# Attention loop of an mLSTM block: loads of the next head ordered behind all splits, output end behind the next weighing

## The chip, the core and the metric

The kernel runs on one core of a Trainium2 chip as one launch. Its time is device time in microseconds (us), as the median of several runs; the profile is one further execution under the hardware profiler. The engines are named as in the profile: PE (matrix multiplications; its weight loads are PEld), DVE (VectorE), ACT (ScalarE), POOL (GpSimd) and SP (SyncE, which here only starts DMAs).

## What is computed

One layer of a diffusion backbone on 512 latent tokens of width 1024 with 256 context tokens. Its parts are an adaLN-modulated RMSNorm, two token mixers on the normalised input (a bidirectional mLSTM with 4 heads of 256 and a Hyena long convolution), a gated merge, an output projection and a SwiGLU. The change lies in the mLSTM. For one head and one direction it is, chunk by chunk:

```python
b = cumsum(log_f)
logD = where(tril, b[t] - b[s] + log_i[s], NEG)
m_t = max(b + m, max(logD))
s = einsum("td,sd->ts", q, k) * exp(logD - m_t)
num = einsum("ts,sd->td", s, v) + a * einsum("vk,tk->tv", C, q)
den = sum(s) + a * einsum("k,tk->t", n, q)
h = num / max(abs(den), exp(-m_t))
```

The kernel does it without chunks: for a head, six blocks of 128 keys (four latent, two of the context), all at once, with a decay weight for each block, query and direction. Then each head is normalised over its 256 channels, multiplied by an output gate, and goes to the next projection.

## The kernel before, in words

All matrix products are made of fp32 values split into a high and a low half. `split` (L214) lets ACT copy the high half (L215) and DVE subtract it to get the low half (L216); `mm3` (L233) then makes a product of three matmuls: high by high (L234), high by low (L235), low by high (L236). Raw tiles come by SP's DMAs into a buffer "wr", of which there are four (L182); a load of the next raw tile can start when the split of the tile four before it is done.

The loop over the heads (from L1373) runs, for head h (0 to 3; the third head is h = 2), in this order:

- `load_head(h + 1)` (L912) starts the loads of Q (one tile) and K (two halves) of the next head and splits them into uh, ul and K. They are traced inside `issued_behind(weighed)`, which orders their instructions, on each engine, behind the last multiply of the weighing of head h; it adds no wait.
- `values(h, 0)` (L970) multiplies the weighted scores of the forward direction by V (vh, vl): four output tiles, each followed by the small division steps (ACT L981 and L985, DVE L982, L983).
- `decay(h + 1, 1)` (L874) fills four banks by matmuls (L882, L884), and ACT makes exponentials of them into the tiles dx and dy (L888); `decay(h + 1, 0)` was traced before it.
- `beside` (L1361) adds an independent piece: a tile of the Hyena projection wph (`ph_tiles`, L1318; a load into "wr", its split into wh and wl, 24 matmuls, a DVE step L1326, a store), and steps over the modulation weights wada (L373, on DVE, from the same four buffers).
- `late` (L1367) is the output end of head h - 1 (`head_out`, L1006): eight transposes on PE into two banks (L1011), an ACT copy of each bank (L1014), a DVE step with the gate (L1015), a split (ACT L220, DVE L221) and stores.
- `weigh(h + 1)` (L949): six products of six matmuls of K and Q; after each, two DVE multiplies (L961) put the scores into the exponentials (tiles dx and dy) and free the bank. Products, decay and output end share one set of four banks; `values` and the wph tile have four others.
- `values(h, 1)` for the backward direction, then `load_values(h + 1)` (L926, V of the next head), `halves` (L964, the splits of dx and dy), another `beside`, and `head_norm` (L989, with a power on POOL, L997).

The order on each engine is what the scheduler makes of this code: it goes by the order written, the priorities and the `issued_behind` and `behind` marks. Each engine runs its own list in order, so an instruction that waits holds up all that stand behind it on that engine.

Of the kernel before, what the change touches and what calls it, by code (L numbers as in the profile page):

```python
# [160 lines left out]
def build(nc, tc, I, out, dbg=None):  # L161
# [24 lines left out]
    def T(p, shape, dt=F32, tag=None, bufs=None):  # L186
        uid[0] += 1
        p = HOME.get(tag, p)
        bufs = BUFS.get(tag, bufs)
        kw = {} if bufs is None else {"bufs": bufs}  # L190
        nm = f"{tag or 't'}_{uid[0]}"
        return p.tile(list(shape), dt, tag=tag or nm, name=nm, **kw)
# [9 lines left out]
    def bank(p=None):  # L202
        return T(p or psH, [128, 512], F32, "bank")
# [10 lines left out]
    def split(hi, lo, x):  # L214
        act.activation(hi, x, AF.Copy)  # L215
        dve.tensor_sub(lo, x, hi.bitcast(F32))  # L216
# [16 lines left out]
    def mm3(o, wh, wl, xh, xl, first, last):  # L233
        pe.matmul(o, wh, xh, start=first, stop=False)  # L234
        pe.matmul(o, wh, xl, start=False, stop=False)  # L235
        return pe.matmul(o, wl, xh, start=False, stop=last)  # L236
# [342 lines left out]
    def behind(lag=0):  # L579

        return tc.issue_after(tails[-1 - lag])
# [285 lines left out]
    def parts(dt=F32):  # L867
        return T(PM_, [128, 10, 128], dt, "dy"), T(PM_, [128, 8, 128], dt, "dx")

    def piece(w, d, s):  # L870
        t0, n, i, off = PIECE[d][s]
        return w[i][:, off : off + n]
# [32 lines left out]
    def staged(src, n, hi, lo, a=None):  # L905
        t = T(PW, [128, WMAX], F32, "wr")[:, :n]
        if a:
            t = t.rearrange("p (a b) -> p a b", a=a)
        dma(t, src)
        split(hi, lo, t)  # L910

    def load_head(h):  # L912

        kh, kl = (T(PT, [128, 2048], F32R, "K")[:, :1536].rearrange("p (a b) -> p a b", a=2) for _ in range(2))
        qh, ql = T(PT, [128, 2, SEQ], F32R, "uh"), T(PT, [128, 2, SEQ], F32R, "ul")

        staged(qd[:, 2 * h : 2 * h + 2], 2 * SEQ, qh[:], ql[:], 2)
        if h == 0:
            fill(next(cf))
        for i in range(2):  # L920
            staged(kd[:, 2 * h + i], SEQ + CTX, kh[:, i], kl[:, i])
        return (qh, ql), (kh, kl)

    weighed, valued = [], []

    def load_values(h):  # L926
        Vh, Vl = T(PM_, [128, 6, NV], F32R, "vh"), T(PM_, [128, 6, NV], F32R, "vl")
        gp.memset(Vh[:, :, 256:257].bitcast(F32), 1.0)
        gp.memset(Vh[:, :, 257:258].bitcast(F32), 0.0)
        gp.memset(Vl[:, :, 256:258].bitcast(F32), 0.0)  # L930
        n0 = len(nc.cur_bb.bb.instructions)
        for b, n in ((0, 4), (4, 2)):
            staged(vd[:, h, b : b + n], 256 * n, Vh[:, b : b + n, :256], Vl[:, b : b + n, :256], n)
        valued[:] = last_of(nc.cur_bb.bb.instructions[n0:])
        return Vh, Vl

    def last_of(traced):

        ends = {i.engine: i for i in traced if i.engine in (nc.vector.engine, nc.scalar.engine)}
        return list(ends.values())  # L940

    @contextmanager
    def issued_behind(ends):
        with ExitStack() as stack:
            for i in ends:
                stack.enter_context(tc.issue_after(i))
            yield

    def weigh(h, qq, kk, Dm):  # L949

        (qh, ql), (kh, kl) = qq, kk
        for s in (4, 5, 0, 1, 2, 3):
            ps = bank()
            tk = slice(128 * s, 128 * s + 128)
            for i in range(2):
                mm3(ps[:], kh[:, i, tk], kl[:, i, tk], qh[:, i], ql[:, i], i == 0, i == 1)
            for d in range(2):
                t0, n = PIECE[d][s][:2]
                dst = piece(Dm[d], d, s)
                sv = ps[:, 128 * t0 : 128 * (t0 + n)].rearrange("p (a b) -> p a b", a=n)  # L960
                m = dve.scalar_tensor_tensor(dst, sv, 1.0 / 64, dst, op0=ALU.mult, op1=ALU.mult)  # L961
        weighed[:] = [m.ins]

    def halves(Dm):  # L964
        wh, wl = parts(F32R), parts(F32R)
        for i in (1, 0):
            split(wh[i][:], wl[i][:], Dm[i][:])
        return wh, wl

    def values(h, d, W, V, den, hs):  # L970
        (wh, wl), (Vh, Vl) = W, V
        for t in range(4):
            ps = bank(psG)
            src = [4, 5] + [s for s in range(4) if (s <= t if d == 0 else s >= t)]
            for j, s in enumerate(src):
                b = t - PIECE[d][s][0]
                m = mm3(ps[:, :NV], piece(wh, d, s)[:, b], piece(wl, d, s)[:, b], Vh[:, s], Vl[:, s], j == 0, j == len(src) - 1)
            tails.append(m.ins)
            dn = den[:, d, t : t + 1]
            with tc.high_priority(PR[0]):  # L980
                act.activation(dn, ps[:, 256:257], AF.Abs)  # L981
                dve.tensor_tensor(dn, dn, G["em"][:, d, t, h : h + 1], op=ALU.max)  # L982
                dve.reciprocal(dn, dn)  # L983
                if d == 0:
                    act.activation(hs[:, t], ps[:, :256], AF.Copy, scale=dn)  # L985
                else:
                    dve.scalar_tensor_tensor(hs[:, t], ps[:, :256], dn, hs[:, t], op0=ALU.mult, op1=ALU.add)
# [12 lines left out]
    def head_gate(h):  # L1000
        o = [T(PM_, [128, SEQ], F32, "s2") for _ in range(2)]
        for i in range(2):
            dma(o[i][:], od[:, 2 * h + i])
        return o
# [223 lines left out]
    def fill(n):  # L1228
        for _ in range(n):
            if fills:  # L1230
                fills.pop(0)()
# [72 lines left out]
    def reload(src, hi, lo, ks=range(KT)):  # L1304
        xs = ([], [])
        for k in ks:
            xs[0].append(hi())
            xs[1].append(lo())
            load_halves(xs[0][-1][:], xs[1][-1][:], both(src, k))
        return xs  # L1310
# [20 lines left out]
    L = load_head(0)  # L1331
    fill(next(cf))
    V = load_values(0)
    sel = T(PM_, [128, 32], F32R, "sel")
# [9 lines left out]
    def steps(n):  # L1344
        for _ in range(n):
            background()

    Dm = [decay(0, d) for d in range(2)]
    fill(next(cf))
    weigh(0, L[0], L[1], Dm)  # L1350
    fill(next(cf))
    W = [halves(Dm[d]) for d in range(2)]
    fill(next(cf))
# [7 lines left out]
    def beside(h, i):  # L1361
        for _ in range(PHN[h][i]):
            with issued_behind(valued if i == 0 else ()):
                next(ph)
        steps(ST[h])

    def late(keep=False):  # L1367
        if done:
            with behind():
                ends.extend(head_out(*done.pop(), keep))  # L1370

    ends = []
    for h in range(NH):  # L1373
        last = h == NH - 1
        den = T(PM_, [128, 2, 4], F32, "den", 2)
        hs = T(PM_, [128, 4, 256], F32, "hs", 2)
        if last:
            sp_ = [T(PT, [128, 2048], F32R, "K") for _ in range(2)]
            parts_ = [[v[:, 512 * j : 512 * j + 512] for j in range(4)] for v in sp_]
            for i, tag in enumerate(("uh", "ul")):  # L1380
                v = T(PT, [128, 2, SEQ], F32R, tag)
                parts_[i] += [v[:, 0], v[:, 1]]
            its = [iter(v) for v in parts_]
            hm = reload(hmd, lambda: next(its[0]), lambda: next(its[1]), range(4))
        else:
            with issued_behind(weighed):
                L = load_head(h + 1)
            with behind():
                D0 = decay(h + 1, 0)
        values(h, 0, W[0], V, den, hs)  # L1390
        if not last:
            with behind():
                Dm = D0, decay(h + 1, 1)
            if h == 0:
                fill(len(fills))
            beside(h, 0)
            late()
            weigh(h + 1, L[0], L[1], Dm)
        values(h, 1, W[1], V, den, hs)
        if last:  # L1400
            late(True)
        else:
            V = load_values(h + 1)
            W = [halves(Dm[d]) for d in range(2)]
            beside(h, 1)
        with tc.high_priority(PR[0] if last else 0):
            head_norm(hs)
        done.append((h, hs, head_gate(h)))
# [8 lines left out]
    with behind():  # L1417
        ends = head_out(*done.pop(), True)
# [369 lines left out]
```

## Time and profile before

| | |
|---|---|
| runs, median of 3 | 1206.57 us (1204.78 to 1208.85) |
| the profiled execution's own time | 1202.72 us |
| its span | 1201.0 us |
| PE busy | 1167.7 us, 97% |
| DVE busy | 933.1 us, 78% |
| ACT busy | 561.8 us, 47% |
| POOL busy | 92.3 us, 8% |

PE is busy in almost every slice of the span, so the profile is read from what PE waits for. The granted clock has a mean of 0.995 of full speed (2.4 GHz). Busy times of the other engines are averages over stages: in the attention loop DVE is nearly full.

### The profile page before, as it was taken

To read this page: it belongs to the slowest core of one execution; us is meant where nothing else is said; L and a number is where in the kernel's file an instruction comes from. 1 tells how busy PE (TensorE), PEld (TensorE's weight loads), DVE (VectorE), ACT (ScalarE), POOL (GpSimd) and SP (SyncE) were. 2 spreads that over 40 slices of the span, in tenths; PEclk is the share of its full clock that TensorE was granted. 3 is DMA by queue.
4 is the path that set the end of the run, shared out by engine and by line. 5 is a ranking of instruction groups with operands and counts; after the bars stand their busy time and mean duration, and the time that the engine had idled before them with its cause. 6 is when DMAs were issued, how large, how long until landed. Compare 5 with 4: busy or idle time off the path is not lost.

```text
span 1201.0 us, 18193 instructions
## 1 busy us (share of the span) xinstructions
PE 1167.7 (97%) x6992; PEld 1028.5 (86%) x6992; DVE 933.1 (78%) x1503; ACT 561.8 (47%) x875; POOL 92.3 (8%) x175
## 2 busy tenths in 40 slices
PE   4999999999999999999999999999999999999997
PEld 2799988988888888888788988879999999998886
DVE  6967798987989999899648887685878987897332
ACT  3763465754554455444756643233433443362221
POOL 0011110110000010101132131000000000000000
PEclk9899999999999999999999999999999999999998
DMA  9745343454245342434685587793323323357312
GB/s 344 258 141 178 142 163 117 143 207 155 86 140 184 115 153 93 175 110 136 215 257 180 175 252 239 261 328 134 121 71 105 106 83 111 106 185 248 98 49 70
DMA packets 64135, 193.31 MB, mean 161 GB/s; under 512 B 8872, under 2 KB 12720, under 8 KB 61488
## 3 DMA queue, kind: packets, MB, share of 16 engines
q1 hardware_dynamic: 51536, 150.20, 37.5%
q0 software_dynamic: 12512, 41.95, 9.8%
q8 instruction: 55, 0.90, 0.3%
q14 instruction: 32, 0.26, 0.1%
HBM read 156.47 MB, written 35.65 MB: 160 GB/s over the span
## 4 chain that ended last, share of the span: by engine, by line
PE 86%; DMA 5%; DVE 5%; issue 1%; ACT 1%; POOL 1%; SPq 0%; DVEq 0%; POOLq 0%; ACTq 0%
PE bank L234 25%; PE bank L235 25%; PE bank L236 24%; DMA wr<-in_wada 2%; PE bank L1558 2%; PE bank L661 2%; PE bank L662 2%; PE bank L663 2%; DVE wl L216 1%; DVE wr L373 1%; DMA mats<-in_mats 1%; PE bank L617 1%; PE bank L464 1%; PE bank L465 1%; DMA hb<-in_dftf 1%
## 5 line engine op out<-in xcount | busy, mean ns | idle before, releaser
L215 ACT ACTIVATE wh<-wr 128x1024 fp32r<-128x1024 f32 (+3 forms) x195 | 195.1, 1005 | 340.8 <-PE bank L235 224.1
L234 PE MATMUL bank<-hTh,wh 128*128 128x512 f32 (+1 forms) x912 | 338.2, 372 | 2.0 <-ACT hTh L1113 2.0
L235 PE MATMUL bank<-hTl,wh 128*128 128x512 f32 (+1 forms) x912 | 337.8, 370 | 2.2 <-DVE hTl L1119 2.2
L236 PE MATMUL bank<-hTh,wl 128*128 128x512 f32 (+1 forms) x912 | 337.1, 370 | 0.0
L216 DVE TENSOR_TENSOR wl<-wr,wh 128x1024 fp32r<-128x1024 f32 (+3 forms) x195 | 223.1, 1153 | 98.6 <-ACT wh L215 96.9
L234 PEld LDWEIGHTS bank<-hTh,wh 128*128 128x128 f32 x912 | 172.9, 190 | 29.6 <-ACT hTh L1113 2.2
L235 PEld LDWEIGHTS bank<-hTl,wh 128*128 128x128 f32 x912 | 172.8, 189 | 29.1 <-DVE hTl L1119 2.5
L236 PEld LDWEIGHTS bank<-hTh,wl 128*128 128x128 f32 x912 | 172.7, 189 | 28.2
L235 PE MATMUL bank<-big,wh 128*128 128x256 f32 (+1 forms) x314 | 101.6, 324 | 1.2 <-DVE big L216 1.2
L234 PE MATMUL bank<-big,wh 128*128 128x256 f32 (+1 forms) x314 | 101.9, 324 | 0.2 <-ACT big L215 0.2
L236 PE MATMUL bank<-big,wl 128*128 128x256 f32 (+1 forms) x314 | 101.4, 323 | 0.0
L235 PEld LDWEIGHTS bank<-big,wh 128*128 128x128 f32 x314 | 59.8, 190 | 6.4 <-DVE big L216 1.8
L234 PEld LDWEIGHTS bank<-big,wh 128*128 128x128 f32 x314 | 59.7, 190 | 5.4 <-ACT big L215 0.8
L236 PEld LDWEIGHTS bank<-big,wl 128*128 128x128 f32 x314 | 59.7, 190 | 4.5
L373 DVE SCALAR_TENSOR_TENSOR wr<-wr,crow 128x1024 f32<-128x1024 f32 x32 | 38.7, 1221 | 23.4 <-DMA wr<-in_wada 23.3
L215 ACT ACTIVATE hb<-hb 128x512 fp32r<-128x512 f32 (+1 forms) x49 | 36.5, 767 | 32.9 <-DVE hb L469 18.1
L234 PE MATMUL bank<-uh,wh 128*128 128x256 f32 (+1 forms) x164 | 51.1, 311 | 0.0
L235 PE MATMUL bank<-ul,wh 128*128 128x256 f32 (+1 forms) x164 | 51.1, 311 | 0.0
L236 PE MATMUL bank<-uh,wl 128*128 128x256 f32 (+1 forms) x164 | 51.1, 311 | 0.0
L216 DVE TENSOR_TENSOR hb<-hb,hb 128x512 fp32r<-128x512 f32 (+1 forms) x49 | 40.5, 860 | 2.0 <-ACT hb L215 1.8
L663 PE MATMUL bank<-wh,hTl 128*128 128x256 f32 (+1 forms) x128 | 36.4, 284 | 0.0
L661 PE MATMUL bank<-wh,hTh 128*128 128x256 f32 (+1 forms) x128 | 36.4, 284 | 0.0
(407 smaller groups left out, 2418.0 us busy)
## 6 DMA issues: line engine op xcount, KB each, us to landing
wr<-in_win SPq DMA_DIRECT2D x64, 512.0 KB, 3.6
wr<-in_w SPq DMA_DIRECT2D x60, 512.0 KB, 3.5
wr<-in_wada SPq DMA_DIRECT2D x32, 512.0 KB, 4.7
Kd<-K POOLq DMA_DIRECT2D x8, 1024.0 KB, 4.7
K<-Kd SPq DMA_DIRECT2D x8, 1024.0 KB, 6.3
wr<-in_wv SPq DMA_DIRECT2D x8, 512.0 KB
gmd<-s POOLq DMA_DIRECT2D x16, 256.0 KB, 2.5
wr<-in_wph SPq DMA_DIRECT2D x8, 512.0 KB, 3.8
```

The source lines that it names most:

```text
L215: act.activation(hi, x, AF.Copy)
L216: dve.tensor_sub(lo, x, hi.bitcast(F32))
L234: pe.matmul(o, wh, xh, start=first, stop=False)
L235: pe.matmul(o, wh, xl, start=False, stop=False)
L236: return pe.matmul(o, wl, xh, start=False, stop=last)
L373: dve.scalar_tensor_tensor(w, w, 1.0, crow[:], op0=ALU.mult, op1=ALU.mult, accum_out=s)
L464: pe.matmul(ps[:], lhs, w4h, start=True, stop=False)
L465: pe.matmul(ps[:], lhs, w4l, start=False, stop=True)
L661: pe.matmul(o, xh, wh, start=bool(k == 0), stop=False)
L662: pe.matmul(o, xh, wl, start=False, stop=False)
L663: m = pe.matmul(o, xl, wh, start=False, stop=bool(k == KT - 1))
L1558: m = pe.matmul(ps, w[:, k], half(h2[x][k], hf), start=n == 1, stop=n == 3 * KT)
```

## The change

`halved` holds the last ACT and the last DVE instruction of the V load and of `halves` of a head. The next iteration orders its Q and K loads' instructions behind these too; for h = 0 it is empty, so the loads of head 1 keep their place and those of heads 2 and 3 move. And `late()` is called after `weigh(h + 1)`; that moves something for h = 1 and h = 2.

```diff
--- before.py
+++ after.py
@@ -1369,7 +1369,7 @@
             with behind():
                 ends.extend(head_out(*done.pop(), keep))
 
-    ends = []
+    ends, halved = [], []
     for h in range(NH):
         last = h == NH - 1
         den = T(PM_, [128, 2, 4], F32, "den", 2)
@@ -1383,7 +1383,7 @@
             its = [iter(v) for v in parts_]
             hm = reload(hmd, lambda: next(its[0]), lambda: next(its[1]), range(4))
         else:
-            with issued_behind(weighed):
+            with issued_behind(weighed + halved):
                 L = load_head(h + 1)
             with behind():
                 D0 = decay(h + 1, 0)
@@ -1394,14 +1394,16 @@
             if h == 0:
                 fill(len(fills))
             beside(h, 0)
+            weigh(h + 1, L[0], L[1], Dm)
             late()
-            weigh(h + 1, L[0], L[1], Dm)
         values(h, 1, W[1], V, den, hs)
         if last:
             late(True)
         else:
+            n0 = len(nc.cur_bb.bb.instructions)
             V = load_values(h + 1)
             W = [halves(Dm[d]) for d in range(2)]
+            halved = last_of(nc.cur_bb.bb.instructions[n0:])
             beside(h, 1)
         with tc.high_priority(PR[0] if last else 0):
             head_norm(hs)
```

No instruction is added or removed. DVE at the second head (h = 1), in the order before. vl is the V of that head, wl the tile of wph, K the second half of K of the third head:

```order
L216 TENSOR_TENSOR vl_6180<-wr_6188,vh_6179 128x2x256
L216 TENSOR_TENSOR wl_6445<-wr_6443,wh_6444 128x1024
L1326 SCALAR_TENSOR_TENSOR s_1074_6246<-s_1074_6246,bank_6248 128x512
L996 TENSOR_SCALAR rs_6277<-mv_6276 128x1
L994 BN_STATS bst_6283<-hs_5886 128x6
L216 TENSOR_TENSOR K_6314<-wr_6325,K_6313 128x768
```

The wph tile is split right behind V, K follows. The same place in the changed kernel:

```order
L216 TENSOR_TENSOR K_6314<-wr_6325,K_6313 128x768
L982 TENSOR_TENSOR den_6311<-den_6311,em_1972 128x1
L995 BN_AGGR mv_6292<-bst_6291 128x2
L994 BN_STATS bst_6299<-hs_5886 128x6
L983 RECIPROCAL den_6311<-den_6311 128x1
L996 TENSOR_SCALAR rs_6293<-mv_6292 128x1
L995 BN_AGGR mv_6300<-bst_6299 128x2
L373 SCALAR_TENSOR_TENSOR wr_6478,modT_78<-wr_6478,crow_5518 128x1024
L216 TENSOR_TENSOR wl_6445<-wr_6443,wh_6444 128x1024
```

wl has moved behind the second half of K, small division and norm steps and a wada step (L373).

ACT at the same place, before; dy and dx are the exponentials of the third head:

```order
L215 ACTIVATE vh_6179<-wr_6188 128x2x256
L215 ACTIVATE wh_6444<-wr_6443 128x1024
L888 ACTIVATE dy_6329<-bank_6331,ad_1908 128x128 x4
L888 ACTIVATE dx_6330<-bank_6338,ax_1910 128x512 x2
L981 ACTIVATE den_6311<-bank_6349 128x1
```

The exponentials follow one another. In the changed kernel:

```order
L215 ACTIVATE vh_6179<-wr_6188 128x2x256
L888 ACTIVATE dy_6329<-bank_6331,ad_1908 128x128 x3
L215 ACTIVATE K_6313<-wr_6325 128x768
L888 ACTIVATE dy_6329<-bank_6331,ad_1908 128x128
L981 ACTIVATE den_6311<-bank_6349 128x1
L888 ACTIVATE dx_6330<-bank_6338,ax_1910 128x512 x2
L985 ACTIVATE hs_6312<-bank_6349,den_6311 128x256
L981 ACTIVATE den_6311<-bank_6363 128x1
L215 ACTIVATE wh_6444<-wr_6443 128x1024
```

The second half of K is split between them, and wh has moved behind a part of the exponentials.

DVE at the third head (h = 2), before; s are tiles of the output end, dx the exponentials of the fourth head, wl tiles of wph:

```order
L1326 SCALAR_TENSOR_TENSOR s_1195_6874<-s_1195_6874,bank_6876 128x512
L216 TENSOR_TENSOR wl_7381<-wr_7379,wh_7380 128x1024
L1015 SCALAR_TENSOR_TENSOR s_1200_6916<-s_1165_6732,s_1200_6916 128x512
L1015 SCALAR_TENSOR_TENSOR s_1201_6923<-s_1166_6733,s_1201_6923 128x512
L961 SCALAR_TENSOR_TENSOR dx_6755<-bank_6930,dx_6755 128x512
L221 TENSOR_TENSOR s_1200_6916<-s_1200_6916,s_1165_6732 128x512
L221 TENSOR_TENSOR s_1201_6923<-s_1201_6923,s_1166_6733 128x512
L961 SCALAR_TENSOR_TENSOR dx_6849<-bank_6930,dx_6849 128x512
L961 SCALAR_TENSOR_TENSOR dx_6755<-bank_6939,dx_6755 128x512
L961 SCALAR_TENSOR_TENSOR dx_6849<-bank_6939,dx_6849 128x512
L216 TENSOR_TENSOR wl_7419<-wr_7417,wh_7418 128x1024
```

The output end stands in front of the multiplies. In the changed kernel:

```order
L1326 SCALAR_TENSOR_TENSOR s_1195_6874<-s_1195_6874,bank_6876 128x512
L961 SCALAR_TENSOR_TENSOR dx_6755<-bank_6906,dx_6755 128x512
L216 TENSOR_TENSOR wl_7381<-wr_7379,wh_7380 128x1024
L961 SCALAR_TENSOR_TENSOR dx_6849<-bank_6906,dx_6849 128x512
L961 SCALAR_TENSOR_TENSOR dx_6755<-bank_6915,dx_6755 128x512
L961 SCALAR_TENSOR_TENSOR dx_6849<-bank_6915,dx_6849 128x512
L961 SCALAR_TENSOR_TENSOR dy_6754<-bank_6924,dy_6754 128x512
```

One multiply stands ahead of wl, the others right behind it; the output end follows after the last multiply of the weighing.

## Rows read from the trace of the kernel before

**Rows 1.** Page, part 1: busy us (share of the span) and number of instructions.

```profile
PE 1167.7 (97%) x6992; PEld 1028.5 (86%) x6992; DVE 933.1 (78%) x1503; ACT 561.8 (47%) x875; POOL 92.3 (8%) x175
```

**Rows 2.** PE's waits: line, waited for: us, times, longest.

```profile
PE bank L234 <- DVE dx L961: 1.4, 1, 1.4
...
PE bank L234 <- ACT s L1014: 0.9, 1, 0.9
```

**Rows 3.** Timeline, PE, third head: start, us, engine, line, operation [idle before].

```profile
689.73 1.03 PE L1011 MATMUL bank<-mats,hs 128*128 128x128 f32 x8
...
693.13 0.39 PE L236 MATMUL bank<-uh,K 128*128 128x512 f32 x1
694.42 0.50 PE L234 MATMUL bank<-uh,K 128*128 128x512 f32 x1 [0.90 <-ACT s L1014]
...
697.06 0.39 PE L236 MATMUL bank<-uh,K 128*128 128x512 f32 x1
698.80 0.47 PE L234 MATMUL bank<-uh,K 128*128 128x512 f32 x1 [1.35 <-DVE dx L961]
...
701.64 0.28 PE L234 MATMUL bank<-vh,dx 128*128 128x258 f32 x1
...
713.65 0.52 PE L234 MATMUL bank<-vh,dx 128*128 128x258 f32 x3
714.01 0.29 PE L235 MATMUL bank<-vl,dx 128*128 128x258 f32 x1
```

**Rows 4.** Timeline, DVE, the same stretch.

```profile
693.83 1.23 DVE L216 TENSOR_TENSOR wl<-wr,wh 128x1024 fp32r<-128x1024 f32 x1 [3.20 <-ACT wh L215]
694.97 1.29 DVE L1015 SCALAR_TENSOR_TENSOR s<-s,s 128x512 f32<-128x512 f32 x2
696.17 0.68 DVE L961 SCALAR_TENSOR_TENSOR dx<-bank,dx 128x512 f32<-128x512 f32 x1
...
697.97 1.88 DVE L961 SCALAR_TENSOR_TENSOR dx<-bank,dx 128x512 f32<-128x512 f32 x3
...
704.20 0.16 DVE L982 TENSOR_TENSOR den<-den,em 128x1 f32<-128x1 f32 x1 [0.63 <-ACT den L981]
...
713.11 0.69 DVE L216 TENSOR_TENSOR vl<-wr,vh 128x512 fp32r<-128x512 f32 x1
```

**Rows 5.** Timeline, ACT, the same stretch.

```profile
692.73 1.06 ACT L215 ACTIVATE wh<-wr 128x1024 fp32r<-128x1024 f32 x1 [2.23 <-DMA wr<-in_wph]
```

**Rows 6.** Timeline, SP's queue, the same stretch.

```profile
688.76 0.33 SPq L255 DMA_DIRECT2D wr<-in_wph  x1
```

**Rows 7.** Timeline, PE, second head.

```profile
648.50 0.74 PE L882 MATMUL bank<-rrow,sel 128*128 128x512 f32 x3
...
649.55 0.40 PE L236 MATMUL bank<-hTh,wl 128*128 128x512 f32 x1
...
655.36 0.47 PE L234 MATMUL bank<-uh,K 128*128 128x512 f32 x1
```

**Rows 8.** Window: length; PE, PEld, DVE, ACT, POOL busy; clock, DMA share, GB/s.

```profile
693.00:714.00 21.00, 18.74 (x108) 16.01 (x107) 19.50 (x37) 10.70 (x16) 6.66 (x15) 1.00 0.81 268
```

**Rows 9.** Timeline, DVE, second head.

```profile
629.48 1.22 DVE L216 TENSOR_TENSOR ul<-wr,uh 128x1024 fp32r<-128x1024 f32 x1
...
638.16 1.21 DVE L216 TENSOR_TENSOR vl<-wr,vh 128x1024 fp32r<-128x1024 f32 x1
...
639.68 0.68 DVE L216 TENSOR_TENSOR vl<-wr,vh 128x512 fp32r<-128x512 f32 x1
...
646.03 1.19 DVE L373 SCALAR_TENSOR_TENSOR wr<-wr,crow 128x1024 f32<-128x1024 f32 x1
```

**Rows 10.** Timeline, SP's queue, second head.

```profile
630.76 0.32 SPq L909 DMA_DIRECT2D wr<-kd  x1
```

**Rows 11.** Page, part 6: DMA issues, number, KB each, median us to landing.

```profile
wr<-in_wada SPq DMA_DIRECT2D x32, 512.0 KB, 4.7
```

**Rows 12.** The tile wr: its loads over the whole kernel.

```profile
DMA to landing us min/median/max: 2.9/3.6/7.9
```

## The prediction

> **What bounds the kernel now.** I read the busy table of the page first, then PE's waits, then the timeline of the attention stretch engine by engine. PE is busy 97% of the span [rows 1], so a change of order that removes no instruction can only win back time in which PE stands still: 1201.0 - 1167.7 = 33.3 us in all. Inside the loop over the heads, from the second on, PE stops twice, 1.4 us behind a VectorE multiply of L961 and 0.9 us behind a ScalarE copy of L1014 [rows 2]. Both lie in one place: the weighing of the fourth head, run while the third head is in work [rows 3]. Weighing and output end share four banks, and two of them are held by the eight transposes of the output end until L1014 has read them; the first two products of the weighing fill the other two, and the third needs one of those.
>
> How the stops come about can be read across the engines. The eight transposes run at 689.73, but the L1014 that reads them starts on ACT only after wh, a split of a weight tile, for which ACT waited 2.23 us on its DMA [rows 5]. That DMA was issued at 688.76 [rows 6]. So the third product waits until 694.42. On DVE wl stands in front of L1015 and of the dx multiplies; it starts after 3.20 us of idling at 693.83, the first multiply of the first weighing bank comes behind two L1015 [rows 4], and the second one, which frees the bank, behind two L221. PE's fifth product so waits until 698.80.
>
> **The change part by part.** No instruction is added or dropped; two orders change.
>
> *The output end behind the weighing.* It acts for heads 1 and 2, whose transposes then run after 36 weighing matmuls. At the second head PE does not stop between transposes and weighing in the trace (weighing starts at 655.36, right behind them [rows 7], and no wait of PE follows), so L1014 reads the banks in time there and the swap is worth nothing. At the third head the two stops can go. Their size by start to start: 694.42 - 693.13 = 1.29 and 698.80 - 697.06 = 1.74 [rows 3], of which 0.23 each is the ordinary step of such a matmul (a product is six matmuls, and the two from 694.42 to 697.06 + 0.23 took 2.87 us, 0.24 each with their start); so 1.06 + 1.51 = 2.57 us is the ceiling of the whole gain, 0.2% of the span.
>
> A new wait replaces part of it. With the transposes gone, PE starts weighing at 689.73. A product takes 1.38 (six steps of 0.23) to 1.43 us (with the start, from the 2.87 for two), so the fifth, the first to need a bank again, is reached at 689.73 + 4 x 1.38 = 695.25, or at 695.45 by the longer. Its bank is freed by the second dx multiply, which in the changed order stands behind wl. The wl split still hangs on the same DMA, so it runs 693.83 to 694.97 [rows 4], and the multiply behind it ends at 694.97 + 0.60 = 695.57 (three L961 in a row take 1.88 [rows 4], 0.60 a step). PE waits 0.1 to 0.3 for it; with the releases between engines, for which no row stands by itself, I take 0.6 for the whole stop. The weighing then ends at 701.64 - 2.57 + 0.6 = 699.67: 1.97 us earlier.
>
> How much of this reaches the end? The next thing PE needs is the V of the fourth head, and DVE makes it last of all. From 693.00 to 714.00 DVE is busy 19.50 of 21.00 us [rows 8], and after 693.83 it stands still once, 0.63 us at 704.20; its last split of V starts at 713.11 and ends at 713.80, and PE takes its first lo half at 714.01 [rows 3, 4], 0.21 us later. In the new order the same instructions stand between 693.83 and that split but one: a single dx multiply, 0.60 us, moves ahead of wl into the idle 3.20. V is thus ready 0.60 us earlier, and 1.23 if the idle 0.63 goes too. PE can therefore gain 0.21 + 0.60 = 0.81 to 0.21 + 1.23 = 1.44 us at that point, and loses the rest of its 1.97 in a new wait in front of the first value product of the fourth head. I take 1.1, the middle.
>
> *K and Q splits behind V and the halves.* The loads keep their order on SP, but the second half of K waits for another buffer of the four: before it was issued when ul was split, 630.76, now when the first split of V is done, 638.16 + 1.21 = 639.37 [rows 9, 10]. SP is in order, so the wph tile, the wada row and the next V load stand behind it. The wph tile waits for the second V split (639.68 + 0.68 = 640.36), the wada row for ul, which now follows V: 640.36 + 1.22 = 641.58. With the landing of 4.7 us that the page gives for wada [rows 11], L373 can run at 641.6 + 4.7 = 646.3, ends at 647.5, and wl, now behind it, at 647.5 + 1.2 + some queueing = 649.0. PE wants this wl at 649.55 [rows 7]: 0.5 us spare, where in the order of before the tile was split right behind V. The K half itself lands at 639.5 + 3.6 = 643.1 [rows 12] and its ACT split stands in the middle of the decay exponentials, the last of which I work out for about 648.3; PE wants their last bank for the next decay with the three L882 from 648.50 [rows 7]: also close. At the third head the same chain has some 3 us to spare. So I cost this part at nothing, covered by 0.5 us; if the cover is gone it costs what the DMA is late.
>
> The rows bear on that: the loads of these tiles land 2.9 us after issue at the least, 3.6 in the middle and 7.9 at most over the whole kernel [rows 12], so the bounds of this part are 0 (it cannot gain: PE stops at no load of Q or K in this stretch) and, with 5.5 to 7.9 in place of 4.7, 0.3 to 2.7 us lost at the second head. I take 0, near which the median row lies. The Trainium skill ("DMA: Bandwidth & Descriptors", section "Issuing engines are not separate DMA queues") says that DMAs started from different engines run on the same 16 engines and interleave; it speaks against the change, for the K half, the tile, the wada row, V and the output stores now fall in one stretch, and by it the loss would lie at the upper end. No row before shows them together.
>
> *Sum.* -1.1 + 0 = -1.1 us on the profiled execution: span 1201.0 to 1199.9, its own time 1202.72 to 1201.6. The runs shown have a median of 1206.57, 3.85 above the profiled execution, and 1204.78 to 1208.85 among themselves, so the forecast on their scale is 1206.57 - 1.1 = 1205.5 us.
>
> **The rivals.** *Full gain.* The V splits are not what PE waits for, since ACT and DVE both close their gaps: then the 1.97 us stay, and if wl comes early enough to spare the new wait, 2.57: 1204.6 to 1204.0. For it: the 0.63 us idle gap on DVE follows PE, so an earlier PE moves it. Against it: DVE is nearly full for 20 us, and only 0.60 us of it moves.
>
> *Nothing.* The weighing is faster but the value products of the fourth head start where they did: 1206.6. For it: V is 0.2 us ahead of PE today. It would take that the moved transposes, whose L1014, L1015 and L221 now come after the weighing and before V, cost DVE what the multiply gave back.
>
> *Slower.* The wl split of the wph tile at the second head is late. Place: PE's first L236 of the tile, at 649.55; price: what a landing exceeds 4.7 + 0.5 = 5.2 us by, so 0.3 to 2.7 at 5.5 to 7.9 us, and up to 3 if the decay's exponentials are late as well; it decides against the gain when the landing exceeds 4.7 + 0.5 + 1.1 = 6.3 us. At a landing of 7.2 us PE waits 7.2 - 5.2 = 2.0 and the time is 1206.57 - 1.1 + 2.0 = 1207.5; at the far end, with the exponentials' 3 us, 1208.5. For it: five transfers fall together. Against it: the median of the tiles is 3.6.
>
> **How the numbers follow.** Forecast (gain 0.8 to 1.4) 0.50, full gain 0.13, nothing 0.15, slower 0.22. None of the cases moves the kernel by more than 0.3%, 3.6 us, which is about what a measurement of it tells from no change; the spread of its three runs, 4.07 us, can. From the gaining cases, which are 2.5 to 1 us short of that bound, I give 0.13 to faster; from the slower case, 1 to 2 short of it at its far end, 0.09 to slower; the rest, 0.78, is the same. The range: 1204.0 and 1208.5 are the ends of the cases, widened below by nearly half the spread of the runs and above by only 0.3, since the slower case reaches its far end only if all is late: 1202.2 to 1208.8.
>
> **What would show it.** Right: in the changed trace PE goes from the wph tile into the weighing at the third head without its 0.9 us stop, the dx multiply runs between 691 and 693 in DVE's idle time, a stop of 0.3 to 0.6 us stands before the fifth product, and a new stop behind the vl split opens the value products of the fourth head about 1 us earlier than 713.65. At the second head the wl split ends just before PE's L236. Wrong: PE stops at the second head in front of the wph tile or of the decay's masks (then the load order costs more than the swap gives), or a fall of more than 2.6 us, for which the two stops leave no room.

## The result and the profile after

The changed kernel is slower: 1207.12 us median (1205.17 to 1209.39, 14 runs) beside 1205.34 us (1202.15 to 1208.85, 14 runs) of the kernel before, a ratio of 1.0019 with a 95% interval of 1.0011 to 1.0027, so 2.3 us of about 1205. I had forecast 1205.5 us, which was 1.1 less than the 1206.57 that the kernel before had in three runs: the time lies in the range, and the direction was wrong. The profiled execution has a span of 1204.3 us and its own time is 1206.12.

The page's first part says that no engine does more work than in [rows 1]; PE is busy 0.1 us longer:

```profile
PE 1167.8 (97%) x6992; PEld 1028.0 (85%) x6992; DVE 933.1 (77%) x1503; ACT 561.0 (47%) x875; POOL 92.0 (8%) x175
```

So the time is in the waits. PE's waits from 640 to 780 us of the changed kernel (line, waited for: us, times, longest):

```profile
PE bank L236 <- DVE wl L216: 1.5, 2, 1.1
PE bank L234 <- ACT den L981: 1.2, 1, 1.2
PE bank L234 <- DVE dx L961: 0.6, 1, 0.6
PE bank L234 <- DVE hs L987: 0.4, 1, 0.4
PE bank L235 <- DVE vl L216: 0.2, 1, 0.2
PE bank L234 <- DVE s L1470: 0.2, 1, 0.2
```

Of the two waits of [rows 2] the one behind L1014 is gone and the one behind dx is smaller; the others are new. Where they are, in the timeline of PE (start, us, engine, line, operation, [idle before]):

```profile
649.58 0.50 PE L236 MATMUL bank<-hTh,wl 128*128 128x512 f32 x1 [0.42 <-DVE wl L216]
...
696.10 0.47 PE L234 MATMUL bank<-uh,K 128*128 128x512 f32 x1 [0.65 <-DVE dx L961]
...
712.60 0.36 PE L234 MATMUL bank<-vh,dx 128*128 128x258 f32 x1 [0.39 <-DVE hs L987]
713.20 0.36 PE L235 MATMUL bank<-vl,dx 128*128 128x258 f32 x1 [0.24 <-DVE vl L216]
...
722.96 0.39 PE L234 MATMUL bank<-vh,dx 128*128 128x258 f32 x1 [1.18 <-ACT den L981]
...
767.70 0.47 PE L234 MATMUL bank<-K,wh 128*128 128x512 f32 x1 [0.24 <-DVE s L1470]
769.47 0.50 PE L236 MATMUL bank<-K,wl 128*128 128x512 f32 x1 [1.06 <-DVE wl L216]
```

The first lies at the wph tile of the second head, the second before the fifth product of the weighing, the next two where the value products of the fourth head begin (against [rows 3], 713.65 and 714.01, which had no wait), and the 1.18 us in the middle of these products. The last two are at the first tile of the merge, after the heads.

A table helps more than the list, since a wait also costs the slower start behind it and a late PE may wait less later. It has the start of the same PE instruction in several profiles, less its start in the profile of before, all shifted so that they agree at the second head's masks (648.05 in before; from 600 us to there no two profiles drift apart). "Before 2" is a second profile of the kernel before, the other columns are the experiments below.

| us against before | after | after 2 | before 2 | E1 | E2 | E3 | E4 | E5 | E8 | E9 | E10 |
|---|---|---|---|---|---|---|---|---|---|---|---|
| third head, tile before the weighing (684.26) | +0.67 | +0.99 | +0.77 | -0.03 | +0.46 | +0.84 | 0.00 | -0.04 | -0.03 | +0.10 | +1.03 |
| third head, tile after the weighing (708.17) | -1.28 | -1.58 | +0.31 | -2.71 | +0.71 | -1.04 | -0.67 | -2.92 | -2.92 | -0.03 | -0.97 |
| fourth head, first value products (714.25) | -0.18 | -0.48 | +0.31 | -1.50 | +1.09 | +0.10 | -0.67 | -1.82 | -1.82 | -0.03 | +0.11 |
| merge begins (744.85) | +1.24 | +0.99 | +0.31 | +0.18 | +1.09 | +0.13 | +0.99 | -1.82 | -1.82 | -0.03 | +0.09 |
| first tile after it (836.89) | +3.60 | +3.78 | +0.76 | +2.22 | +2.92 | +2.31 | +3.27 | +0.14 | -1.80 | +1.01 | +0.06 |
| measured, ratio less 1, of 1205 us | +2.3 | | | +0.6 | +1.4 | +0.2 | +3.3 | -1.8 | -3.0 | -1.8 | -0.7 |

In the changed kernel PE loses 0.67 us at the second head, wins 1.95 in the weighing of the fourth head, and then loses 2.52 in the fourth head's own products: 1.10 where they begin and 1.42 behind den. The two profiles of before differ by up to 0.8 us at one place, so smaller entries of single profiles decide nothing.

*The loss at the second head.* DVE there, in the changed kernel:

```profile
647.16 1.23 DVE L373 SCALAR_TENSOR_TENSOR wr<-wr,crow 128x1024 f32<-128x1024 f32 x1 [1.45 <-DMA wr<-in_wada]
...
648.31 1.22 DVE L216 TENSOR_TENSOR wl<-wr,wh 128x1024 fp32r<-128x1024 f32 x1
```

wl waits behind L373, and L373 behind its row of wada, which SP had issued at 641.41. wl was finished at 649.53, PE wanted it at 649.0 (649.55 in before, [rows 7], in a profile that runs 0.55 us later).

*The loss in the fourth head.* ACT there, first in before, then in the changed kernel: wh is a wph tile and then the first wpm tile (the weights of the merge), den the small step of the value products that lets a bank go:

```profile
716.73 1.06 ACT L215 ACTIVATE wh<-wr 128x1024 fp32r<-128x1024 f32 x1 [0.48 <-DMA wr<-in_wph]
...
718.76 1.06 ACT L215 ACTIVATE wh<-wr 128x1024 fp32r<-128x1024 f32 x1 [0.91 <-DMA wr<-in_wpm]
719.72 0.15 ACT L981 ACTIVATE den<-bank 128x1 f32<-128x1 f32 x1
```

```profile
717.84 1.06 ACT L215 ACTIVATE wh<-wr 128x1024 fp32r<-128x1024 f32 x1 [2.33 <-DMA wr<-in_wph]
...
721.43 1.06 ACT L215 ACTIVATE wh<-wr 128x1024 fp32r<-128x1024 f32 x1 [2.48 <-DMA wr<-in_wpm]
722.39 0.15 ACT L981 ACTIVATE den<-bank 128x1 f32<-128x1 f32 x1
```

PE's 1.18 us are the wait for this den: it stood behind the split of a tile that PE takes up only at 745.54, and the split waited for a DMA. The DMAs were not issued later: SP issues these two tiles at 712.09 and 713.08, and in before, which runs 0.55 us later, at 712.83 and 713.82. They took longer: ACT, which waited for each, starts the two splits 5.8 and 8.4 us behind the issue in place of 3.9 and 4.9. What else was on the DMA engines is seen on POOL. The output end stores the outputs of the first two heads (hmd<-s), and the iteration of the last head loads them back for the merge (`reload`, K<-hmd, four loads of 256 KB for each head). First before, then the changed kernel:

```profile
696.62 1.14 POOL L222 DMA_DIRECT2D hmd<-s  x2 [5.12 <-ACT s L220]
...
701.88 0.54 POOL L227 DMA_DIRECT2D K<-hmd  x1 [2.98 <-PE bank L236]
...
705.66 0.58 POOL L228 DMA_DIRECT2D K<-hmd  x1
```

```profile
703.39 1.10 POOL L222 DMA_DIRECT2D hmd<-s  x2 [1.69 <-ACT s L220]
...
705.05 1.20 POOL L223 DMA_DIRECT2D hmd<-s  x2 [0.57 <-DVE den L983]
710.69 0.54 POOL L227 DMA_DIRECT2D K<-hmd  x1 [4.43 <-DMA hmd<-s]
...
711.93 0.54 POOL L227 DMA_DIRECT2D K<-hmd  x1 [0.52 <-DMA hmd<-s]
712.57 1.17 POOL L228 DMA_DIRECT2D K<-hmd  x2
```

In before the stores of the second head's output go at 696.62 and all eight reloads from 701.88 to 706.2. Now the stores are seven microseconds later, since the output end stands behind the weighing, and the four reloads that read what they stored begin at 710.69, just as SP issues the wph and the wpm tile. The windows from 712 to 720 us (us, busy PE, PEld, DVE, ACT, POOL, clock, DMA share, GB/s), first of before, then of the changed kernel:

```profile
712.00:720.00 8.00, 8.00 (x61) 7.69 (x61) 7.49 (x22) 2.88 (x6) 3.02 (x4) 1.00 0.59 171
```

```profile
712.00:720.00 8.00, 7.37 (x59) 7.02 (x59) 6.61 (x22) 1.76 (x4) 4.54 (x7) 1.00 1.02 305
```

The share of the DMA engines, as the profile sums it, goes from 0.59 to 1.02. The granted clock is 1.00 (2.4 GHz) in both.

### The profile page after: what moved, and what is told of

Same layout as the page of the kernel before. It is cut to its first block, busy times and chain, and to the rows that moved or that the text cites. A ratio compares the mean times of both kernels' runs of the same rounds, so it can differ in the third digit from the quotient of the medians.

```text
span 1204.3 us, 18192 instructions
## 1 busy us (share of the span) xinstructions
PE 1167.8 (97%) x6992; PEld 1028.0 (85%) x6992; DVE 933.1 (77%) x1503; ACT 561.0 (47%) x875; POOL 92.0 (8%) x175
## 4 chain that ended last, share of the span: by engine, by line
PE 82%; DVE 7%; DMA 6%; issue 2%; ACT 2%; POOL 0%; SPq 0%; DVEq 0%; POOLq 0%; ACTq 0%
PE bank L234 23%; PE bank L235 23%; PE bank L236 23%; DMA wr<-in_wada 3%; PE bank L1560 2%; PE bank L662 2%; PE bank L661 2%; PE bank L663 2%; DMA wr<-in_wph 1%; DVE wl L216 1%; DVE wr L373 1%; DMA wr<-in_wpm 1%; PE bank L617 1%; PE bank L464 1%; DVE hs L987 1%
## 5 line engine op out<-in xcount | busy, mean ns | idle before, releaser
L236 PE MATMUL bank<-hTh,wl 128*128 128x512 f32 (+1 forms) x912 | 336.6, 369 | 0.4 <-DVE wl L216 0.4
L236 PEld LDWEIGHTS bank<-hTh,wl 128*128 128x128 f32 x912 | 172.4, 189 | 28.9 <-DVE wl L216 0.9
L236 PE MATMUL bank<-big,wl 128*128 128x256 f32 (+1 forms) x314 | 101.4, 323 | 0.0
L236 PEld LDWEIGHTS bank<-big,wl 128*128 128x128 f32 x314 | 59.7, 190 | 4.6
L373 DVE SCALAR_TENSOR_TENSOR wr<-wr,crow 128x1024 f32<-128x1024 f32 x32 | 38.7, 1221 | 25.5 <-DMA wr<-in_wada 25.4
L236 PE MATMUL bank<-uh,wl 128*128 128x256 f32 (+1 forms) x164 | 51.1, 311 | 0.0
L662 PE MATMUL bank<-wl,hTh 128*128 128x256 f32 (+1 forms) x128 | 36.5, 285 | 0.0
```

The source lines that it names most:

```text
L373: dve.scalar_tensor_tensor(w, w, 1.0, crow[:], op0=ALU.mult, op1=ALU.mult, accum_out=s)
L662: pe.matmul(o, xh, wl, start=False, stop=False)
```

## The experiments

**Theory A:** the loss in the fourth head is made by the reloads, which come with the moved output end and collide with the tiles that SP loads; the load order costs only what PE stops at the second head. **Theory B:** the loads of Q and K, now behind V, have put the tile loads behind. Times are compared with runs of the kernel before on the same chip.

**E1, the output end moved alone.** Of the change only the swap:

```diff
-            with issued_behind(weighed + halved):
+            with issued_behind(weighed):
```

> The output end behind the weighing, with the loads ordered as before the change. Theory A (the moved output end pushes its stores, and the reloads of them, onto the transfers that feed the fourth head): the second head runs as before, without the 0.4 us stop in front of the wph tile; the third head's weighing wins 2.0 us again; in the fourth head's value products PE still stops some 1.2 us behind ACT, because wph and wpm tiles land 1 to 3 us late, and the tile loads stay about 2.4 us behind until the merge; in all about 1.5 us slower than before. Theory B (the loads of Q and K, now behind V, put the tile loads behind): no stop in the fourth head, 1 to 2 us faster than before.

Measured: 1205.86 us beside 1204.77, ratio 1.0005 (0.9995 to 1.0015). The second head is as before, and the weighing wins 2.7 us, more than in the changed kernel: the stop before its fifth product is absent. Then the fourth head gives all of it back. PE there:

```profile
712.06 0.36 PE L234 MATMUL bank<-vh,dx 128*128 128x258 f32 x1 [0.49 <-DVE hs L987]
712.66 0.36 PE L235 MATMUL bank<-vl,dx 128*128 128x258 f32 x1 [0.24 <-DVE vl L216]
...
722.62 0.39 PE L234 MATMUL bank<-vh,dx 128*128 128x258 f32 x1 [1.40 <-ACT den L981]
```

So the stop behind den comes with the output end, against theory B. But the swap alone costs 0.6 and not 1.5 us: the load order must cost more than A gave it.

**E2, the load order alone.** `late()` back ahead of `weigh`:

```diff
-            weigh(h + 1, L[0], L[1], Dm)
             late()
+            weigh(h + 1, L[0], L[1], Dm)
```

> The loads of Q and K ordered behind V and the halves, with the output end ahead of the weighing as before. Theory A: PE stops once more than before, 0.4 us (0.7 with its slower start) in front of the wph tile at the second head; the two stops of the third head's weighing stay; none in the fourth head; 0.5 to 1.0 us slower than before. Theory B: stops in the fourth head and at the merge, 2.5 to 4 us slower.

Measured: 1206.52 us, ratio 1.0012 (1.0003 to 1.0021), 1.4 us slower: above A's bound and below B's. No stop behind den in the fourth head, as A has it. At the second head the stop is another: 0.2 us in front of the transposes, behind the exponentials of ACT (0.46 us in the table). And the two stops of the third head's weighing together grow from 2.25 to 2.54 us, which A had not:

```profile
655.75 0.98 PE L1011 MATMUL bank<-mats,hs 128*128 128x128 f32 x7 [0.21 <-ACT dx L888]
...
696.36 0.50 PE L234 MATMUL bank<-uh,K 128*128 128x512 f32 x1 [1.68 <-ACT s L1014]
700.75 0.47 PE L234 MATMUL bank<-uh,K 128*128 128x512 f32 x1 [0.86 <-DVE dx L961]
```

In [rows 3] these were 0.90 and 1.35, so the first grows and the second shrinks.

**E3, the changed kernel with the four reloads held back** until the last power of the third head's norm (the list `normed` holds it):

```diff
-            hm = reload(hmd, ..., range(4))
+            hm = reload(hmd, ..., range(2))
+            with issued_behind(normed):
+                h1 = reload(hmd, ..., range(2, 4))
```

> The changed kernel, with the four reloads of the second head's output (1 MB) issued behind the last power of the third head's norm, some 12 us later, behind the wph and wpm tiles. Theory A: the tiles land in some 4 us again, PE's 1.2 us stop behind ACT in the fourth head and the 1.1 us stop at the merge go; 2 to 3 us faster than the changed kernel, so 0 to 1 us faster than before. Theory B, or a theory by which the fourth head stops because DVE and ACT come late with the moved output end: the stops stay, within 0.5 us of the changed kernel.

Measured: 1205.22 us, ratio 1.0002 (0.9993 to 1.0010), where the changed kernel has 1.0019: 2.0 us come back, and the stop behind den is gone. POOL issues the reloads from 726.45, and the window from 712 to 720 us reads:

```profile
712.00:720.00 8.00, 7.36 (x53) 6.71 (x52) 7.38 (x23) 0.65 (x2) 2.68 (x4) 1.00 0.73 225
```

The wpm split on ACT now waits 0.20 us for its DMA in place of 2.48, but the wph split ahead of it waits longer than in the changed kernel, 2.94 in place of 2.33:

```profile
720.18 1.06 ACT L215 ACTIVATE wh<-wr 128x1024 fp32r<-128x1024 f32 x1 [2.94 <-DMA wr<-in_wph]
...
721.49 1.06 ACT L215 ACTIVATE wh<-wr 128x1024 fp32r<-128x1024 f32 x1 [0.20 <-DMA wr<-in_wpm]
```

(This profile runs 1.7 us later there than that of the changed kernel; the wpm split begins 8.0 us behind the start of the value products here, 9.6 there and 5.1 in before.) So the tiles do not land in some 4 us again, as A expected, and what is won is a margin: counted from the 714.25 row of the table, den starts after 5.5 us in before, 8.9 in the changed kernel and 7.2 in E3, and in each of the four profiles that stop there (the changed kernel twice, E1, E4) its start less the stop is 7.7. The stop is gone by half a microsecond. A part of the lateness is therefore not the four reloads. One more transfer moves with the output end: the second load of the third head's output gate (od, L1003, a tile of 128x512), into the set of buffers that the output end's tiles use. SP issues it at 700.6 in before and here just ahead of the wph tile:

```profile
712.51 0.32 SPq L1003 DMA_DIRECT2D s<-od  x1
713.89 0.33 SPq L255 DMA_DIRECT2D wr<-in_wph  x1
```

No run holds this load apart, so what it costs is not shown. The stops at the merge stayed, 0.92 and 1.07 us in this profile, against A.

**E4, the kernel before with its reloads made late.** Output end and loads stand where they stood; all eight reloads, 2 MB, are issued behind the memsets of V:

```diff
-            hm = reload(hmd, ..., range(4))
+            with issued_behind(cleared):
+                hm = reload(hmd, ..., range(4))
```

> The kernel before, with all eight reloads (2 MB) issued behind the memsets of V, from about 708.5 instead of 702 us, and nothing else moved. Theory A: the wph and wpm tiles land 1 to 3 us later, PE stops in the fourth head's value products behind ACT, and the time is 1 to 3 us longer than before, though output end and loads stand where they stood. Theory B: no stop, the time of before within 0.5 us.

Measured: 1208.08 us, ratio 1.0027 (1.0018 to 1.0036), 3.3 us slower, a little more than the 1 to 3 of A. ACT and PE in the fourth head:

```profile
719.74 1.06 ACT L215 ACTIVATE wh<-wr 128x1024 fp32r<-128x1024 f32 x1 [4.27 <-DMA wr<-in_wph]
...
721.62 1.06 ACT L215 ACTIVATE wh<-wr 128x1024 fp32r<-128x1024 f32 x1 [0.77 <-DMA wr<-in_wpm]
```

```profile
723.16 0.39 PE L234 MATMUL bank<-vh,dx 128*128 128x258 f32 x1 [1.43 <-ACT den L981]
```

The same stop at the same den, in a kernel whose orders on PE, DVE, ACT and SP are those of before, row by row. E3 takes the stop away by moving reloads, and E4 makes it by moving reloads: that settles theory A for this stop. The wph tile, split at 716.73 in before, is split three microseconds later. The Trainium skill ("DMA: Bandwidth & Descriptors", section "Issuing engines are not separate DMA queues") says that DMAs of several engines run on the same 16 DMA engines and interleave; here POOL's reloads hold up SP's tiles, so these runs agree with it. The size is not explained in full: up to the merge the profile shows 0.99 us, and the runs 3.3.

**E5, the swap with the reloads held back,** loads of Q and K as before the change (E1 with the edit of E3).

> The output end behind the weighing, the loads of Q and K as before the change, and the four reloads of the second head's output held back. Theory A: the third head's weighing wins 2.5 to 2.8 us, 0.6 to 1.4 of it is lost again to V in the fourth head, no 1.2 us stop behind ACT there, and PE reaches the merge 0.8 to 1.5 us earlier than before; whether that reaches the end depends on the row loads of wada, which pace the merge: 0 to 1.5 us faster than before. Theory B (only the load order matters): the time of the swap alone, 1205.9 us, within 0.5.

Measured: 1203.23 us beside 1205.60, ratio 0.9985 (0.9976 to 0.9994), 1.8 us faster than before, somewhat more than expected, and 2.4 less than E1 by the ratios. PE's stops in the heads that are left:

```profile
711.12 0.35 PE L234 MATMUL bank<-vh,dx 128*128 128x258 f32 x1 [0.45 <-DVE hs L987]
711.63 0.38 PE L235 MATMUL bank<-vl,dx 128*128 128x258 f32 x1 [0.15 <-DVE vl L216]
```

The weighing gains 2.9 us, 1.1 of it goes back at the start of the fourth head's value products, and 1.8 stays to the merge, which is what the runs measure. The kernel before with the four reloads held back and nothing else was not run; but up to the merge it could win nothing by that, since PE stops there only in the weighing [rows 2].

**E6 and E7, before and changed kernel once more,** each profiled a second time, unchanged. Theory C: the wada rows pace the merge, and the first profile of before had no stop there by luck.

> The kernel before, unchanged, for a second profile of it. Theory C (its first profile was an execution in which the merge had no stop, while most have one, since the wada rows that pace it land 1 to 2 us earlier or later from one execution to the next): stops of together 1 to 2 us at the first merge tile, behind wl and behind the DVE step ahead of it, and a span of 1202.5 to 1204. Rival: no stop at the merge, as in the first profile; then the changed orders, all of them, cause it.

> The changed kernel, unchanged, for a second profile. Theory A: the same stops at the second head (0.4 us), before the fifth product of the weighing (0.6), and in the fourth head (0.4, 0.2 and 1.2 us), since they come from the order; the merge's stops may differ by 1 us and more.

Measured: 1203.80 us (span 1202.0) and 1207.55 us (span 1205.7). The changed kernel shows the same stops in the same places (0.7, 0.4, 0.2 and 1.2 us in the heads), all but the 0.65 us before the fifth product, which so lies on the edge. Before has one stop at the merge now, smaller than C had it:

```profile
767.91 0.50 PE L236 MATMUL bank<-K,wl 128*128 128x512 f32 x1 [0.56 <-DVE wl L216]
```

**E8 and E9, one wada step moved from the first tile of the merge to the last,** on E5 and on the kernel before:

```diff
-        steps(1)
+        steps((0, 1, 1, 1, 1, 1, 1, 2)[d])
```

> As the swap with the reloads held back, and one of the wada steps of the merge moved from its first tile to its last, so that on DVE one row load less stands in front of the first merge tile. Theory C: the stops at the first merge tile (2 us in all kernels but the first profile of before) go, 1 to 2 us faster than the same kernel without it, and so faster than before. Rival (the merge waits for the wpm tiles or y2d themselves): the stops stay, no change.

> The kernel before with the one wada step of the merge moved to its last tile. The second profile of before has 0.6 us of stop at the first merge tile, the first none: 0 to 1 us faster than before. If it is 2 us faster or more, the fastest kernel so far (0.9975 of before) owes its time to this step and not to the swap; if it is near 1.000, swap and held reloads are worth the rest.

Measured: E8 1201.68 us, ratio 0.9975 (0.9960 to 0.9989), the fastest kernel of the study; E9 1202.81 us, ratio 0.9985 (0.9975 to 0.9995). In E8's profile the stops at the first merge tile (in E5 1.07 us) are gone, which fits C, and E9's has none there either, like the first profile of before. But at the next product, whose tiles (big) the merge makes, E9 stops 2.4 us in all, where the two profiles of before stop 1.3 and 1.1:

```profile
794.52 0.51 PE L234 MATMUL bank<-big,wh 128*128 128x512 f32 x1 [1.33 <-ACT big L215]
795.87 0.50 PE L235 MATMUL bank<-big,wh 128*128 128x512 f32 x1 [0.84 <-DVE big L216]
```

So E9's profile is 1.0 us behind the first one of before (that execution took 1204.26 us, 1.45 above E9's median), though its runs are 1.8 us faster, more than either profile of before had to lose at the first merge tile (0 and 0.56). By the ratios the step gives 1.2 us on E5 and 1.8 on before, and swap with held reloads 1.2 on top of it (0.9985 to 0.9975); for both 1.2 the intervals overlap, so neither is shown. Where E9's runs win it is not shown.

**E10, E8 with the load order of the change:**

> The whole change, with the reloads held back and the wada step moved: the fastest kernel so far, but with the loads of Q and K behind V and the halves. If the load order costs what it cost alone, it is 1 to 1.5 us slower than the fastest, about 0.9985 of before; PE stops 0.4 to 0.7 us in front of the wph tile at the second head and 0.6 before the fifth product of the weighing. If its cost lay only in the lateness that the other two edits take away, it is as fast as the fastest.

Measured: 1203.90 us, ratio 0.9994 (0.9985 to 1.0002), 2.3 us above E8, where 1 to 1.5 was expected. Up to the merge its profile is 1.9 us behind E8's, with the stops at the second head (0.79, expected 0.4 to 0.7) and before the fifth product (0.62, expected 0.6). In all four pairs the load order costs: alone 1.4 us, on the swap 1.7 (1.0019 to 1.0005), on E5 2.0 (1.0002 to 0.9985), on E8 2.3. The first is clear of the noise (1.0003 to 1.0021); in the other three the intervals of the two kernels overlap at their ends, but all four agree in sign.

## Why the prediction was wrong, step by step

*The two stops of the weighing: right in the changed kernel.* 1.97 us were worked out for the third head; 1.95 came (+0.67 to -1.28). The new stop before the fifth product was taken as 0.6 and was 0.65, behind the multiply behind wl, as said.

```profile
691.77 0.68 DVE L961 SCALAR_TENSOR_TENSOR dx<-bank,dx 128x512 f32<-128x512 f32 x1
694.13 1.22 DVE L216 TENSOR_TENSOR wl<-wr,wh 128x1024 fp32r<-128x1024 f32 x1 [1.68 <-ACT wh L215]
695.27 1.88 DVE L961 SCALAR_TENSOR_TENSOR dx<-bank,dx 128x512 f32<-128x512 f32 x3
```

One multiply stands in DVE's idle time and the next behind wl. The margin is small: E1 and E5, with the old load order, lack that stop, and so does the second profile of the changed kernel, while E3 and E10 have it (0.7 and 0.6 us).

*V of the fourth head: right.* "PE can therefore gain ... 0.81 to 1.44 us at that point, and loses the rest of its 1.97": the last split of V began at 712.37, and of the 1.95 us PE keeps 0.85 there (+0.67 to -0.18) and loses 1.10. In E5 it loses 1.10 too, in E3 1.14 (it keeps 0.74). A part of the stop stands behind hs (L987, 0.39 to 0.49 us), which DVE runs just ahead of the last split of V, so it is the same full DVE; I had named V alone.

*The load order at nothing, "covered by 0.5 us": mis-sized.* The cover was not there. The chain was the one worked out (wada row, L373, wl, then PE's L236), but the row that SP issued at 641.41 let L373 start at 647.16, 5.7 us later, in place of 4.7 [rows 11]. PE lost 0.67 us. It is the rival "slower", at its place and with the lower part of its price. And the third head does not have the 3 us to spare that I gave it: in most profiles with the new load order the weighing wins 0.7 to 1.0 us less there (1.9 to 2.0 in after, E3 and E10, 2.7 to 2.9 in E1, E5 and E8), since wl comes too late for the multiply behind it (SP issues that tile at 689.75, some 1.5 us later than [rows 6] when the two profiles are aligned). Up to the merge the pairs of profiles differ by 1.1 to 2.0 us; the runs measured 1.4 to 2.3. So a term put at nothing took by itself all that the swap gives: with the reloads out of the way the whole change is at 1.0002 (E3), not at the gain of 1.1. The forecast had named this stop as a sign of being wrong.

*What was not in the sum: the DMAs of the moved step.* This is the step that failed outright. The output end was followed on PE, ACT and DVE until V; its stores are named once, among the transfers of the second head, and what reads them nowhere. The forecast followed POOL's queue nowhere, though [rows 8] has it 6.66 of 21 us busy. The sum then ended at the first value product, as if PE had nothing to wait for behind it. By the runs the collision costs 2.0 to 2.4 us (E3 against the changed kernel, E5 against E1; in both pairs the intervals do not overlap).

The runs add up along one path: the swap without the collision gives 1.8 us (E5, in place of the 1.1 forecast), the load order takes 2.0 (E5 to E3), the reloads take 2.0 to 2.1 (E3 to the changed kernel), together the +2.3 measured.

*The sum as it should have been:* -1.95 at the weighing, with 1.10 back at V, 0.67 at the second head, and 1.42 for the stop behind den: +1.24 us up to the merge in this profile, +0.99 in the second one. The runs show +2.3 (1.3 to 3.3 by the interval). The rest would have to lie behind the merge's begin, where the two kernels' profiles differ by 2.4 us more (1.24 to 3.60), but where E5 in its profile loses 2.0 as well and is still 1.8 us faster than before in its runs. The first profile of before was one of its fast executions (1202.72 us; median 1205.34). What part of that 2.4 us belongs to the change can't be told from single profiles and stays open.

## What to carry to other kernels

A step that is moved takes its stores along, and with them every load that reads what it stored: look for what these transfers now meet, which can be a stretch of the program that the change does not touch. Small steps that let a bank go should not stand in order behind the split of a tile that is needed much later, because such a split hands the DMA's delay on to the matmuls. When a loop waits in a few places for under a microsecond, every cover below a microsecond counts as nothing, since transfers land one or two microseconds apart from case to case (here 5.7 us behind the issue at the second head, where 4.7 was counted on).

## What the runs showed that I had not expected

Making eight reloads of 256 KB some six microseconds later, with nothing else moved, cost 3.3 us (1.0027), more than the whole change. Moving one wada step out of the first tile of the merge gave 1.8 us (0.9985) to the kernel before, as much as the swap with the reloads held back (E5); both together gave 3.0 us (0.9975).
